# Order-only edges on the accumulating DRAM transfers of a Strassen-like FFN kernel

## The chip, the core and the metric

The kernel runs on one core of a Trainium2 chip. The metric is device time in microseconds, the median of repeated executions of the whole kernel. Engines are named as the profile names them: PE is TensorE (with PEld for its weight loads), DVE is VectorE, ACT is ScalarE, POOL is GpSimd, and SP is the engine that issues most of the DMAs.

## The reference, cut to what matters

The kernel computes one layer: a gated linear attention mixer, then a gated FFN with a short causal convolution, then a last norm. The change lies in the FFN.

```python
def causal_dwconv(u, w, b):          # K = 3
    up = jnp.pad(u, ((0, 0), (K - 1, 0), (0, 0)))
    out = up[:, K - 1:K - 1 + L] * w[K - 1] + b
    for k in range(K - 1):
        out = out + up[:, k:k + L] * w[k]
    return out

def conv_ffn(h, w_up, conv_w, conv_b, w_down):
    u = causal_dwconv(h @ w_up, conv_w, conv_b)
    g, val = jnp.split(u, 2, axis=-1)
    return (jax.nn.silu(g) * val) @ w_down
...
x = x + conv_ffn(rmsnorm(x, ffn_norm_w[i]), ...)
```

There are 2048 tokens of 1024 features, and the FFN is 2816 wide. All data are float32.

## The kernel before

Every large matrix product is made of 7 block products in place of 8 (the scheme of Strassen in Winograd's form). The products are called p1 to p7; sums and differences of blocks are formed ahead of them and after them. Each float32 operand is split into a rounded high part and a rest (`split`, L186 to L189: ACT casts the high part, DVE subtracts it), and `mm3p` (L173 to L184) makes three matmuls of each pair of operands, at L179, L180 and L181.

The FFN has an up part (`phase_u`) and a down part (the last loop of the kernel).

**The up part** goes over the tokens in two halves of 1024, called s = 0 and s = 1, and in each half over 11 groups, g or q = 0 to 10, of two blocks f = 2g and 2g + 1 of 128 FFN features. A group has 14 jobs, seven products in the order `OPS` = p1, p5, p6, p7, p4, p2, p3 with two blocks each; a job is 12 matmuls, so a group is 168. The first matmul of a group's p2 writes a tile `ub`, which is how a group is found in the trace. For every job there is a weight operand:

- `load` (L1198) has SP fetch the four blocks of the weights of each f into tiles `ur`.
- `prep` (L1207) runs five jobs ahead of PE. For p5, p6, p7 and p3 POOL forms sums of blocks: `us` at L1214 (p5), L1217 (p6), L1232 (p3), and `ur` at L1220 (p7). Then ACT casts the result into `uw` and DVE subtracts (L188 and L189).
- PE's results are copied by ACT (`c<-ua`, L1237 for p1 and p6, L1342 for p7). p1, p6, p7 and p4 of a block add up in one PSUM bank `ua`. So PE may start p6 only when ACT has copied p1's result out, and p7 only when p6's has been copied.
- `new_u` (L1240) takes a buffer `u` out of three; its first instruction, at L1243, is a copy of two columns on POOL, which waits for the convolution that held the buffer before. `conv` (L1247) is the convolution: ACT at L1253, DVE twice at L1255, and for the gating half ACT's Silu at L1257. `gated` (L1260) multiplies the two halves on DVE (L1262).

**The operands of the down part** are formed from the results of `gated`. In the second half, POOL makes four sums for each group into SBUF tiles `as` (L1284), and SP writes them out. In the first half, SP writes plain blocks into DRAM tiles `ad` (L1267), and the sums are formed in DRAM: a transfer issued on POOL's queue reads one `ad` tile and adds it to another (`gather`, L1360 to L1363). Four of these belong to each q, and each reads or writes what another one has written:

1. p7 += p5
2. p5 += p4
3. p6 += p5
4. p3 += p6

In the program they are traced during the second half, at jobs 2, 5, 10 and 13 of each group (the table `GATHER`, L1288 and L1296 to L1298); the third and the fourth of the last q are traced in the down part (L1548 and L1550). A scheduler decides where each instruction stands on its engine. It puts an instruction where its inputs are there by its own reckoning, and so the 44 transfers stand on POOL in the first half, right behind the writes that they need.

**Between the halves**, `load_op` (L900, called from L1305) has SP fetch the 28 operand tiles `h_p` of the second half, 512 KB each, while the last group of the first half runs.

**The down part** takes 14 units of 11 steps: p1, p5, p6, p7, p2, p4, p3, each for both halves. SP loads the operands `da` (L1402) eleven steps ahead.

Of the kernel before, what the change touches and what calls it, by code (L numbers as in the profile page):

```python
# [14 lines left out]
ALU = mybir.AluOpType  # L15
# [10 lines left out]
def hybrid_kernel(  # L26
# [17 lines left out]
    nc = tc.nc  # L44
# [67 lines left out]
    def scratch(shape, name):  # L112
        return dr.tile(shape, F32, tag=name, name=name)
# [10 lines left out]
    ad = {(s, o, q): scratch([P, 512], f"ad_{s}_{o}_{q}") for s in range(NS) for o in OPS for q in range(NQ)}  # L124
# [4 lines left out]
    def aux_ps(name):  # L129
        return ps.tile([P, 512], F32, tag="aux", name=name, bufs=4)  # L130
# [66 lines left out]
    halo = cst.tile([P, 2 * NF, 2], F32, name="halo")  # L197
# [984 lines left out]
    def tiles2(ap):  # L1182

        v = ap.rearrange("p (j c k) -> p c j k", c=2, k=P)
        return v[:, 0], v[:, 1]
# [6 lines left out]
    def phase_u():  # L1192
# [47 lines left out]
        def new_u(s, i, f):  # L1240
            c = f + i * NF
            u = pools["us"].tile([P, TS + 2], F32, tag="u", name=f"u_{s}_{c}", bufs=3)
            nc.gpsimd.tensor_copy(u[:, 0:2], halo[:, c, :])  # L1243
            made["u", i, f] = u
            return tiles2(u[:, 2:2 + TS])

# [48 lines left out]
        for k, (s, g, o, f) in enumerate(jobs):  # L1295
            if s == 1 and k % GJ in GATHER:  # L1296
                dst, src, back = GATHER[k % GJ]
                gather(dst, src, g - back)  # L1298
# [27 lines left out]
            elif o == "p5":  # L1326
                c = bank["c", f] = aux_ps(f"uc_{s}_{f}")
                mm3p(c, pairs)
            elif o == "p6":
                a = bank["a", f]  # L1330
                mm3p(a, pairs, first=False, more=True)
                made["u2", f] = copied(f"c2_{s}_{f}", a)
            elif o == "p2":
                pb = mm_ps(f"ub_{s}_{f}")
                mm3p(pb, pairs)
                ev, _ = new_u(s, 0, f)
                nc.vector.tensor_add(ev, tiles1(pb), tiles1(made.pop(("p1", f))))  # L1337
            elif o == "p7":
                a = bank["a", f]
                mm3p(a, pairs, first=False, more=True)  # L1340
                u3 = pools["us"].tile([P, 512], F32, tag="as", name=f"c3_{s}_{f}", bufs=AB)
                nc.scalar.copy(u3, a)  # L1342
                ev, od = new_u(s, 1, f)
                made["ev", f] = ev
                nc.vector.tensor_add(od, tiles1(bank["c", f]), tiles1(u3))
            elif o == "p4":
                a = bank.pop(("a", f))
                mm3p(a, pairs, first=False, more=True)
                nc.scalar.copy(made.pop(("ev", f)), tiles1(a))
                conv(s, 1, f)  # L1350
            else:
                c = bank.pop(("c", f))
                mm3p(c, pairs, first=False, more=True)
                _, od = tiles2(made["u", 0, f][:, 2:2 + TS])
                nc.vector.tensor_add(od, tiles1(c), tiles1(made.pop(("u2", f))))  # L1355
                conv(s, 0, f)
                gated(s, f)


    def gather(o, src, q):  # L1360

        if 0 <= q < NQ:
            nc.gpsimd.dma_start(ad[0, o, q], ad[0, src, q], accum_op=ALU.add, max_dma_last_dim=2048)  # L1363

    units = [(o, s) for o in ("p1", "p5", "p6", "p7", "p2", "p4", "p3") for s in range(NS)]
    steps = [(o, s, q) for o, s in units for q in range(NQ)]
# [163 lines left out]
    for n, (o, s) in enumerate(units):  # L1530
        banks = [(mm_ps if n % 2 == 0 else aux_ps)(f"pd_{o}_{s}_{m}") for m in range(PAIRS)]
        last = n + 1 == len(units)

        def products(q, ms):
            ah, al = aops[o, s, q]
            for m in ms:
                ts = slice(m * P, (m + 1) * P)
                mm3p(banks[m], [((ah[:, ts], al[:, ts]), wops[o, q])], first=(q == 0), last=(q == NQ - 1))

        tail = 5 if last else 0  # L1540
        for q in range(NQ):
            k = n * NQ + q
            d_load(k + DLEAD + DLOAD + 1)
            d_prep(k + DLEAD + 1)
            if n < NS and q < TT:
                load_x1(s * TT + q)
            if n == 0 and q == TT:
                gather("p6", "p5", NQ - 1)  # L1548
            elif n == 1 and q == TT:
                gather("p3", "p6", NQ - 1)  # L1550
            if n == 2 and q == 0:
                nc.sync.dma_start(nwf, final_norm_w.partition_broadcast(P))
            if q < NQ - tail:
                products(q, range(PAIRS))
        for m in range(PAIRS):
            for q in range(NQ - tail, NQ):
                products(q, [m])
            use(o, s, m, banks[m], nwf)
# [31 lines left out]
```

## Time and profile before

| | |
|---|---|
| median of three runs | 2170.98 us (2165.34 to 2174.02) |
| time of the profiled execution | 2172.34 us |
| its span | 2170.3 us |
| PE busy | 2080.6 us (96%) |
| DVE busy | 1627.6 us (75%) |
| ACT busy | 1105.6 us (51%) |
| POOL busy | 688.3 us (32%) |

The profile is that of one execution. A row of a timeline has the start in us, the duration in us, the engine with the line, the operation, and the tiles as out<-in; in brackets stands the idle time of the engine just ahead of it and what ended it. A row of a list of waits has the engine and line that waited, what it waited for, the sum in us, the number of times and the longest one. In names such as `ua<-h_p,uw_p` the numbers are left out.

### The profile page before, as it was taken

To read this page: it belongs to the slowest core of one execution; us is meant where nothing else is said; L and a number is where in the kernel's file an instruction comes from. 1 tells how busy PE (TensorE), PEld (TensorE's weight loads), DVE (VectorE), ACT (ScalarE), POOL (GpSimd) and SP (SyncE) were. 2 spreads that over 40 slices of the span, in tenths; PEclk is the share of its full clock that TensorE was granted. 3 is DMA by queue.
4 is the path that set the end of the run, shared out by engine and by line. 5 is a ranking of instruction groups with operands and counts; after the bars stand their busy time and mean duration, and the time that the engine had idled before them with its cause. 6 is when DMAs were issued, how large, how long until landed. Compare 5 with 4: busy or idle time off the path is not lost.

```text
span 2170.3 us, 28933 instructions
## 1 busy us (share of the span) xinstructions
PE 2080.6 (96%) x9832; PEld 1723.4 (79%) x9832; DVE 1627.6 (75%) x2168; ACT 1105.6 (51%) x2024; POOL 688.3 (32%) x606
## 2 busy tenths in 40 slices
PE   6999999989998998899999997999999999999998
PEld 5888788878887877688787786888888877888886
DVE  8756888799888664678988875988788777457564
ACT  5555755665565775454554543554445533233342
POOL 2000011111111002345446444665665444036010
PEclk9999999999999999999999999999999999999999
DMA  6646684578557899686676679342424567354453
GB/s 220 224 165 212 211 296 139 157 228 300 170 190 261 315 332 363 224 220 157 174 199 155 177 198 294 97 122 83 136 73 122 185 244 281 95 184 160 142 180 115
DMA packets 328357, 423.30 MB, mean 195 GB/s; under 512 B 24446, under 2 KB 183342, under 8 KB 328208
## 3 DMA queue, kind: packets, MB, share of 16 engines
q1 hardware_dynamic: 284336, 346.99, 48.8%
q10 hardware_dynamic: 37536, 62.93, 8.6%
q0 software_dynamic: 6336, 11.54, 3.5%
q8 instruction: 77, 1.26, 0.2%
q14 instruction: 72, 0.59, 0.1%
HBM read 278.23 MB, written 154.66 MB: 199 GB/s over the span
## 4 chain that ended last, share of the span: by engine, by line
PE 56%; DMA 14%; DVE 13%; issue 7%; POOL 4%; ACT 3%; SPq 2%; ACTq 0%; DVEq 0%; POOLq 0%
PE pd_p L180 5%; PE pd_p L181 5%; PE pd_p L179 5%; PE ua L179 4%; PE ua L181 4%; PE ua L180 4%; DVE t L1255 3%; DMA ad_p<-ad_p 3%; PE uc L179 2%; PE uc L181 2%; PE uc L180 2%; PE mp_R L179 2%; PE mp_R L181 2%; PE mp_R L180 2%; PE mp_A L181 1%
## 5 line engine op out<-in xcount | busy, mean ns | idle before, releaser
L179 PE MATMUL ua<-h_p,uw_p 128*128 128x512 f32 x704 | 278.6, 396 | 23.9 <-ACT c L1237 23.9
L1255 DVE SCALAR_TENSOR_TENSOR t<-u,cw,t 128x1024 f32<-128x1024 f32 x176 | 285.3, 1625 | 11.9 <-ACT t L1253 10.9
L180 PE MATMUL ua<-h_p,uw_p 128*128 128x512 f32 x704 | 276.4, 393 | 0.0
L181 PE MATMUL ua<-h_p,uw_p 128*128 128x512 f32 x704 | 276.3, 392 | 0.0
L180 PE MATMUL pd_p<-dw_p,da 128*128 128x512 f32 x616 | 240.3, 390 | 3.4 <-DVE da L189 3.4
L179 PE MATMUL pd_p<-dw_p,da 128*128 128x512 f32 x616 | 240.1, 390 | 0.6 <-DVE u L1337 0.6
L181 PE MATMUL pd_p<-dw_p,da 128*128 128x512 f32 x616 | 240.0, 390 | 0.0
L189 DVE TENSOR_TENSOR da<-da_p,da 128x512 fp32r<-128x512 f32 x154 | 133.7, 921 | 104.5 <-ACT da L188 104.4
L188 ACT CAST da<-da_p 128x512 fp32r<-128x512 f32 x154 | 85.3, 619 | 207.2 <-PE pd_p L181 147.2
L188 ACT CAST uw_p<-us 128x512 fp32r<-128x512 f32 x132 | 82.1, 622 | 203.9 <-POOL us L1217 124.3
L179 PEld LDWEIGHTS ua<-h_p,uw_p 128*128 128x128 f32 x704 | 133.5, 190 | 58.6 <-ACT c L1237 31.5
L189 DVE TENSOR_TENSOR uw_p<-us,uw_p 128x512 fp32r<-128x512 f32 x132 | 136.3, 1038 | 51.7 <-ACT uw_p L188 50.4
L189 DVE TENSOR_TENSOR uw_p<-ur,uw_p 128x512 fp32r<-128x512 f32 x176 | 143.2, 842 | 40.8 <-ACT uw_p L188 40.6
L181 PEld LDWEIGHTS ua<-h_p,uw_p 128*128 128x128 f32 x704 | 133.4, 190 | 28.2
L180 PEld LDWEIGHTS ua<-h_p,uw_p 128*128 128x128 f32 x704 | 133.6, 190 | 27.4
L179 PE MATMUL uc<-h_p,uw_p 128*128 128x512 f32 x352 | 138.1, 392 | 4.5 <-issue 4.5
L1253 ACT ACTIVATE t<-u,cw 128x1024 f32<-128x1024 f32 x88 | 109.7, 1247 | 60.9 <-DVE u L1355 53.0
L180 PE MATMUL uc<-h_p,uw_p 128*128 128x512 f32 x352 | 137.8, 392 | 0.7 <-DVE uw_p L189 0.7
L180 PEld LDWEIGHTS pd_p<-dw_p,da 128*128 128x128 f32 x616 | 115.7, 188 | 28.6 <-DVE da L189 4.7
L181 PE MATMUL uc<-h_p,uw_p 128*128 128x512 f32 x352 | 137.6, 391 | 0.0
L179 PEld LDWEIGHTS pd_p<-dw_p,da 128*128 128x128 f32 x616 | 115.7, 188 | 25.1 <-DVE u L1337 1.0
L181 PEld LDWEIGHTS pd_p<-dw_p,da 128*128 128x128 f32 x616 | 115.7, 188 | 23.8
(278 smaller groups left out, 5340.9 us busy)
## 6 DMA issues: line engine op xcount, KB each, us to landing
ur<-in_ffn_w_up_dram SPq DMA_DIRECT2D x168, 256.0 KB, 4.0
da_p<-ad_p SPq DMA_DIRECT2D x154, 256.0 KB, 4.0
h_p<-hd_p SPq DMA_DIRECT2D x56, 512.0 KB, 8.6
ad_p<-t SPq DMA_DIRECT2D x110, 256.0 KB, 3.2
x<-in_x_dram SPq DMA_DIRECT2D x32, 512.0 KB, 4.7
ch<-in_ffn_w_down_dram SPq DMA_DIRECT2D x61, 256.0 KB, 3.7
hr_A_p<-h1d_p SPq DMA_DIRECT2D x56, 256.0 KB, 2.9
hr_B_p<-h1d_p SPq DMA_DIRECT2D x56, 256.0 KB, 3.3
```

What stands on the lines that cost most here:

```text
L179: nc.tensor.matmul(ps_ap, ah, bl, start=(first and i == 0), stop=False, **kw)
L180: nc.tensor.matmul(ps_ap, al, bh, start=False, stop=False, **kw)
L181: nc.tensor.matmul(ps_ap, ah, bh, start=False, stop=(last and i == len(pairs) - 1), **kw)
L188: nc.scalar.copy(hi, src)
L189: nc.vector.tensor_sub(lo, src, f32(hi))
L1253: nc.scalar.activation(t, u[:, 2:2 + TS], AF.Identity, scale=cw[:, 2, c:c + 1], bias=cw[:, 3, c:c + 1])
L1255: nc.vector.scalar_tensor_tensor(t, u[:, k:k + TS], cw[:, k, c:c + 1], t, op0=ALU.mult, op1=ALU.add)
```

## The change

The copy of `new_u` on POOL is remembered, and each `gather` is traced inside a block that gives it an edge to the last such copy: an edge of order alone, so that the transfer stands behind that copy in POOL's queue and waits for nothing more. Nothing is computed otherwise, and no transfer is added or taken away.

```diff
         def new_u(s, i, f):
...
-            nc.gpsimd.tensor_copy(u[:, 0:2], halo[:, c, :])
+            upool["ins"] = nc.gpsimd.tensor_copy(u[:, 0:2], halo[:, c, :])
...
+    upool = {}
+
     def gather(o, src, q):
 
         if 0 <= q < NQ:
-            nc.gpsimd.dma_start(ad[0, o, q], ad[0, src, q], accum_op=ALU.add, max_dma_last_dim=2048)
+            with tc.issue_after(upool["ins"].ins):
+                nc.gpsimd.dma_start(ad[0, o, q], ad[0, src, q], accum_op=ALU.add, max_dma_last_dim=2048)
```

The order of the instructions on PE, DVE, ACT and SP is the same before and after. On POOL the 44 transfers move, and all else keeps its order. Three places show it; `-` marks what stood there before and `+` what stands there now, and the gather's line is L1363 before and L1366 after. In a name such as `ad_p_3_378` the 3 is the q; 375 to 385 are p7's tiles, 353 to 363 are p5's, 386 to 396 p4's, 364 to 374 p6's and 408 to 418 p3's.

POOL in the first half, at the group that forms the sums for the blocks f = 10 and 11, where the sums of q = 3 stood:

```order
 L1243 COPY u_8_11095<-halo 128x2
-L1363 DMA ad_p_3_378<-ad_p_3_356 128x512
-L1363 DMA ad_p_3_356<-ad_p_3_389 128x512
 L1214 TENSOR_TENSOR us_10_11098<-ur_10_0_10905,ur_10_1_11005 128x512
 L1220 TENSOR_TENSOR ur_10_0_10905<-ur_10_0_10905 128x512
-L1363 DMA ad_p_3_367<-ad_p_3_356 128x512
 L1214 TENSOR_TENSOR us_11_11119<-ur_11_0_10908,ur_11_1_11008 128x512
 L1220 TENSOR_TENSOR ur_11_0_10908<-ur_11_0_10908 128x512
-L1363 DMA ad_p_3_411<-ad_p_3_367 128x512
 L1251 COPY halo<-u_30_11002 128x2
```

All four transfers of a q are gone from between the weight sums.

POOL at the end of the first half, ahead of the first weight sums of the second half (`us_0`):

```order
 L1243 COPY u_43_12939<-halo 128x2
 L1243 COPY u_20_13010<-halo 128x2
-L1363 DMA ad_p_9_384<-ad_p_9_362 128x512
-L1363 DMA ad_p_9_362<-ad_p_9_395 128x512
-L1363 DMA ad_p_9_373<-ad_p_9_362 128x512
-L1363 DMA ad_p_9_417<-ad_p_9_373 128x512
 L1251 COPY halo<-u_42_12913 128x2
 L1251 COPY halo<-u_43_12939 128x2
```

Here the four stood in one row, each behind the one that it needs, and all four are gone.

POOL in the second half, around the weight sums for f = 10 and 11:

```order
 L1243 COPY u_9_14562<-halo 128x2
+L1366 DMA ad_p_3_411<-ad_p_3_367 128x512
 L1217 TENSOR_TENSOR us_10_14544<-us_10_14544,ur_10_0_14364 128x512
+L1366 DMA ad_p_5_380<-ad_p_5_358 128x512
+L1366 DMA ad_p_4_368<-ad_p_4_357 128x512
 L1243 COPY u_32_14760<-halo 128x2
 L1217 TENSOR_TENSOR us_11_14565<-us_11_14565,ur_11_0_14367 128x512
```

Three transfers, of three different q, now stand around the even block's p6 sum; the fourth of a group (p5 += p4) stands two copies further on, behind `u_33` and ahead of `u_10`. A transfer and the one that it needs are now most of a group apart, or, for p7 += p5 and the p5 += p4 of the same q behind it, six instructions of POOL apart.

## The prediction

> **What bounds the kernel now.** I began with the busy time of the engines by stretch, because the change touches one third of the kernel: the first token half, the passage to the second, and the second half.
>
> ```profile
> 920.00:1290.00 370.00, 359.38 (x1558) 292.66 (x1559) 311.18 (x321) 189.07 (x289) 184.84 (x182) 1.00 0.69 179
> 1290.00:1380.00 90.00, 77.57 (x323) 62.71 (x322) 59.30 (x58) 36.08 (x54) 42.13 (x38) 0.94 0.82 253
> 1380.00:1700.00 320.00, 320.00 (x1413) 265.12 (x1412) 267.15 (x253) 156.27 (x233) 195.24 (x137) 1.00 0.34 103
> ```
>
> The columns are the stretch, its length, the busy time of PE, PEld, DVE, ACT and POOL, the granted clock, the share of DMA and GB/s. In the second half PE is busy for all 320 us: it bounds that stage. In the first half PE is idle for 10.6 us of 370 and in the passage for 12.4 us of 90, so something else bounds them. Small gaps also slow the matmuls beside them, so I read what they really cost from the distance of equal places: the first matmul of `ub`, one to a group.
>
> ```profile
> 934.44 0.39 PE L179 MATMUL ub<-h_p,uw_p 128*128 128x512 f32 x1
> ...
> 1290.52 0.39 PE L179 MATMUL ub<-h_p,uw_p 128*128 128x512 f32 x1
> ...
> 1383.89 0.39 PE L179 MATMUL ub<-h_p,uw_p 128*128 128x512 f32 x1
> ...
> 1688.53 0.39 PE L179 MATMUL ub<-h_p,uw_p 128*128 128x512 f32 x1
> ```
>
> The last two are eight groups apart: 304.64 / 8 = 38.08 us for a group when PE never waits. The first two are nine groups apart: 356.08 us, which is 13.4 us over 9 x 38.08. Between them and the second half lie two groups in 93.37 us, 17.2 us over 2 x 38.08. These **30.6 us** are all that can be won here. Next, who waits in the first half:
>
> ```profile
> POOL ad_p L1363 <- DMA ad_p<-ad_p: 76.1, 20, 7.3
> ACT uw_p L188 <- POOL us L1217: 47.2, 18, 5.5
> ...
> POOL ad_p L1363 <- DMA ad_p<-t: 34.3, 9, 3.9
> ...
> PE ua L179 <- ACT c L1237: 8.8, 13, 1.7
> ```
>
> POOL stands for 110 us at its own accumulating transfers, ACT stands for POOL's weight sums, and PE stands 13 times for a copy that ACT makes late. ACT and POOL work in order, so these could be one cause. The chain of waits shows that they are:
>
> ```profile
> 1040.77 3.62 DMA ad_p<-t
> ...
> 1045.00 6.98 DMA ad_p<-ad_p
> ...
> 1052.91 1.60 POOL us L1214
> ...
> 1054.59 2.17 POOL ur L1220
> ...
> 1059.29 1.56 POOL us L1214
> ...
> 1064.52 1.25 POOL us L1217
> ...
> 1072.38 1.27 DVE t L1255
> ...
> 1080.36 3.70 DMA ad_p<-t
> ```
>
> Each row is a start, a duration and what the chain was on. It is a loop with no PE in it: a write of `gated` lands, the first transfer runs for 6.98 us while the second one waits for it at the head of POOL, then come the weight sums, the casts, the convolution and the next write. One turn takes 39.59 us, longer than PE's 38.08. That is the first half's bound. In the passage:
>
> ```profile
> 1288.80 0.84 POOL L1363 DMA_DIRECT2D ad_p<-ad_p  x1 [7.10 <-DMA h_p<-hd_p]
> ...
> 1304.16 1.56 POOL L1214 TENSOR_TENSOR us<-ur,ur 128x512 f32<-128x512 f32 x1
> ...
> 1320.96 0.80 PE L179 MATMUL ua<-h_p,uw_p 128*128 128x512 f32 x1 [7.26 <-ACT c L1237]
> ...
> 1349.96 0.77 PE L179 MATMUL uc<-h_p,uw_p 128*128 128x512 f32 x1 [4.50 <-issue]
> ```
>
> The four transfers of q = 9 stand in a row ahead of the second half's first weight sum; it starts at 1304.16, and 16.8 us later PE has stood for 7.26 us. The 4.50 us at 1349.96 are ahead of p3 of that group; the order of the program has PE wait there for the last operand tiles `h_p`.
>
> **The change part by part.** Nothing is removed but places. *First half:* 40 transfers leave the queue, 4 for each of q = 0 to 9, and the turn loses the waits between them. Take the turn above. Its first L1214 also needs weights that SP fetched behind the same writes:
>
> ```profile
> 1045.11 4.77 SPq L1204 DMA_DIRECT2D ur<-in_ffn_w_up_dram  x5
> ...
> DMA to landing us min/median/max: 6.0/6.1/6.9
> ```
>
> The second row is that of the first four of these loads. They are there from 1051 on, two of them hardly before 1052.9, so I leave the first L1214 where it is. The second L1214 can follow as soon as the L1220 ahead of it ends, at 1054.59 + 2.17 = 1056.76, and not at 1059.29: 2.5 us. The transfer ahead of L1217 goes too, 0.5 us. 39.59 - 3.0 = 36.6 us, under 38.08, so PE bounds again. Of the 13.4 us I take **12.4** as won, 1 us left for groups less regular than this one; the ends are 0 and 13.4.
>
> *Passage:* it has a second cause, and it stays.
>
> ```profile
> 1280.00:1304.00 24.00, 24.00 (x108) 19.87 (x107) 9.53 (x11) 7.24 (x11) 3.10 (x5) 1.00 1.08 323
> ...
> 1289.41 8.42 SPq L1204 DMA_DIRECT2D ur<-in_ffn_w_up_dram  x4
> ...
> DMA to landing us min/median/max: 9.6/11.5/12.2
> ```
>
> The last row is that of these four weight loads. The DMA engines are full (a share of 1.08), since the 28 `h_p` loads run here. The first weight block landed at 1289.41 + 9.6 = 1299 at the earliest, so with the loads as they are the first L1214 can move up by 5 us at most. What helps is that the transfers are DMA work too:
>
> ```profile
> q0 software_dynamic: 6336, 11.54, 3.5%
> ...
> L1363 POOL DMA_DIRECT2D ad_p<-ad_p x44: 805/813/1042, 924.0 to 1349.9; - x44
> ...
> DMA to landing us min/median/max: 3.7/6.0/8.1
> ```
>
> The queue of the transfers took 3.5% of 2170.3 us on all 16 engines, or 1.7 us for each of 44. Four fewer, ahead of 1304, free up to 7 us of a full queue, and then the loads land some 3 to 4 us sooner. After 1304 I count nothing: five transfers go, about as many come. I take 4 to 6 us off the first stop and its slow matmuls, and 2 to 4 off the second: **8 of 17.2**; the ends are 0 and 17.2.
>
> *Second half:* 44 issues come. What one holds POOL for is seen where nothing waits between it and the next instruction:
>
> ```profile
> 1052.37 0.81 POOL L1363 DMA_DIRECT2D ad_p<-ad_p  x1 [6.55 <-DMA ad_p<-ad_p]
> ```
>
> The L1214 behind it starts at 1052.91: 0.54 us. Where three of them come in:
>
> ```profile
> 1502.46 0.52 POOL L1243 COPY u<-halo 128x2 f32<-128x2 f32 x1 [1.21 <-DVE t L1255]
> 1503.01 2.28 POOL L1217 TENSOR_TENSOR us<-us,ur 128x512 f32<-128x512 f32 x1
> 1506.50 0.18 POOL L1243 COPY u<-halo 128x2 f32<-128x2 f32 x1 [1.21 <-DVE t L1255]
> 1507.65 1.68 POOL L1217 TENSOR_TENSOR us<-us,ur 128x512 f32<-128x512 f32 x1 [0.96 <-DVE uw_p L189]
> ...
> 1515.52 0.51 POOL L1243 COPY u<-halo 128x2 f32<-128x2 f32 x1 [3.01 <-ACT t L1253]
> ...
> 1516.38 0.56 ACT L1237 COPY c<-ua 128x512 f32<-128x512 f32 x1
> ...
> 1519.89 0.39 PE L179 MATMUL ua<-h_p,uw_p 128*128 128x512 f32 x1
> ```
>
> The even sum (1503.01) ends 0.54 later, at 1505.83; two issues end at 1506.91; the copy waiting until 1506.50 is 0.4 late; the odd sum still starts at 1507.65, when DVE is done. So it costs nothing on the path. If that cover goes, there is another: the odd sum ended at 1509.33, and through ACT and DVE in order it sets ACT's copy, done at 1516.94, which PE needs at 1519.89. **The margin is 2.95 us.** Behind the transfers on POOL stand only these sums and copies. The fourth stands behind `u_33`, ahead of a copy that waits for DVE anyway. None should wait for the one before it: most of a group lies between them, or, for p5 += p4, the 9 us from 1506 to the copy at 1515.52, against a median landing of 6.0. The DMA engines have room, at a share of 0.34. What the trace of before never shows is two transfers issued with none landed between. I take 0.54 us for the second; it could be as much as the 6 to 7 us of before. *Down part:* SP's queue keeps its order, and its loads of `da` come to the sums only in the third unit (p5), some 60 us after the last matmul of the up part; nothing.
>
> Sum: 2172.34 (the profiled execution; its span is 2170.3, and the median shown, 2170.98, is 1.4 lower) - 12.4 - 8 = 2151.9; from the median it would be 2150.6. I say **2151**.
>
> **The rivals.**
>
> *The loop closes another way (or the passage gives nothing).* The weight loads stand on SP behind the same writes, so the loop still exists: write, `ur` load, sums, cast, convolution. I gave it 36.6 us. If the loads land 1.5 us later than I think, nothing but a part is won. For it: DVE is busy for 311 of 370 us. Against it: the same loop in the second half, where POOL has more to do (195 of 320 us), leaves PE no gap. Price: a win of 4 to 11 us, 2161 to 2168.
>
> *It does not do what it says:* the edges hold only the order, and a transfer might still reach POOL's head unready. But a transfer can now not stand ahead of a copy in the second half, so its sources landed long ago. Price: 2172.
>
> *Slower: three transfers at a time hold POOL.* Should POOL's queue take a transfer only when the one before has landed, as its waits had it until now, then three in a row around the even sum cost 6 us for the second and 6 for the third. The second starts at 1505.8 and the first landed at 1509; the second at 1515, so the odd sum starts at 1515.6 or so instead of 1507.65: 8 us late, 5 over the margin, ten times: + 50 us. With the 20.4 won, 2202. It decides from 2.95 us of lateness on. Against it: the issues took 805 to 1042 ns, not more, but each was alone. Nothing else speaks for it.
>
> *Held by DVE.* POOL's transfers might have to wait for DVE's instructions to end.
>
> ```profile
> L1255 DVE SCALAR_TENSOR_TENSOR t<-u,cw,t 128x1024 f32<-128x1024 f32 x176 | 285.3, 1625 | 11.9 <-ACT t L1253 10.9
> ```
>
> If each of the three waited for one whole such instruction, 1.6 us, the odd sum would start at 1506.91 + 4.9 + 0.18 = 1512.0, 4.3 us late, 1.4 over the margin: 14 us in ten groups, 2166. It decides above 1.1 us each. Against it: the 44 issues had DVE busy for 84% of the time beside them, and the longest took 1042 ns where the median took 813, so 0.2 us each is what the trace bears out. The Trainium skill ("SBUF — State Buffer", in "SBUF: two separate sides") has this as a rule: GpSimd cannot write the descriptors of its own DMAs while a two-port operation of VectorE holds the port that they share, and a DMA of some 620 ns takes some 3100 ns. By that figure, as an estimate from the page, three would cost 7.4 us and ten groups some 40 us. The trace does not agree, with its 1042 ns at most.
>
> **How the numbers follow.** Forecast as above (2145 to 2160): 0.66. The loop or the passage keeps a part (2161 to 2168): 0.17. No effect: 0.06. Held by transfers in flight: 0.08. Held by DVE: 0.03. The range of 2141 to 2166 takes in the whole 30.6 us at one end, and most of the partial case and the hold by DVE at the other; outside are no effect, the transfers in flight and a little of the partial case, 0.18. About 0.5% (10.9 us) is what a measurement of this kernel can tell from no change. Faster than that are the forecast and half the partial case, 0.74; within it the other half, no effect and the hold by DVE, 0.18; slower is 0.08.
>
> **What would show it.** Right: `ub` to `ub` at 38.1 us in the first half; POOL's waits at its transfers near 0; ACT's idle time for `us` in the first half down; one stop or two left in the passage, 7 to 11 us over; in the second half PE still without a gap, and the odd L1217 at most 1 us later. Wrong: a first half still at 39 us or more, with the chain going through `ur` loads; a passage of 93 us as before; POOL standing between the three transfers, and PE waiting for L1237 in the second half.

## The result, and the profile after

| | before | after |
|---|---|---|
| median, measured side by side | 2172.11 us (2165.34 to 2174.02) | 2149.05 us (2146.11 to 2150.57) |
| the profiled execution | 2172.34 us | 2148.77 us |
| its span | 2170.3 us | 2146.8 us |

The ratio is 0.9898, with a 95% interval of 0.9873 to 0.9922: the changed kernel is faster by 1.0%, or 23 us of the medians. The forecast was 2151 us, range 2141 to 2166. In the changed kernel the lines behind `gather` are numbered three higher, so the transfers are at L1366 and the chain sums of the down part, before at L1420, at L1423.

First the busy time by stretch of the changed kernel (stretch, length, busy us of PE, PEld, DVE, ACT, POOL, granted clock, share of DMA, GB/s), with the borders moved to its own stages:

```profile
920.00:1280.00 360.00, 360.00 (x1585) 297.47 (x1584) 316.05 (x319) 189.42 (x288) 171.11 (x146) 1.00 0.55 163
1280.00:1360.00 80.00, 74.05 (x317) 60.23 (x316) 57.68 (x56) 37.76 (x57) 45.33 (x38) 0.98 0.83 250
1360.00:1680.00 320.00, 320.00 (x1413) 264.99 (x1412) 265.10 (x256) 156.51 (x232) 215.74 (x172) 1.00 0.52 128
```

PE no longer has a gap in this stretch: 360 us of 360, where it had been idle for 10.6 of 370. (One stop lies at the edge: 3.08 us at 921.81 before, inside the stretch of before, and 1.92 us at 917.86 after, just outside this one.) In the passage 6 us of gaps are left of 12.4. In the second half POOL works 20 us more and the DMA engines have a share of 0.52 in place of 0.34, and PE is as busy as it was. Then the distances of `ub`, by the timeline of PE in the changed kernel:

```profile
930.51 0.39 PE L179 MATMUL ub<-h_p,uw_p 128*128 128x512 f32 x1
...
1273.64 0.39 PE L179 MATMUL ub<-h_p,uw_p 128*128 128x512 f32 x1
...
1358.20 0.39 PE L179 MATMUL ub<-h_p,uw_p 128*128 128x512 f32 x1
...
1700.92 0.39 PE L179 MATMUL ub<-h_p,uw_p 128*128 128x512 f32 x1
```

The nine groups of the first half take 343.13 us (356.08 before), that is 0.4 over 9 x 38.08. The two groups of the passage take 84.56 (93.37 before), 8.4 over. The nine groups of the second half take 342.72, exactly 9 x 38.08, as before. From the last `ub` to the end of the span there are 445.9 us, and there had been 443.7: the down part has lost 2.2. The rest of the span's difference lies ahead of these places: 2.8 us before the first `ub`, where no transfer stands in either kernel, and 1.1 us in the group after it.

The waits of the changed kernel from 925 to 1285 (who waited, for what, us in sum, times, longest):

```profile
POOL us L1214 <- DMA ur<-in_ffn_w_up_dram: 101.9, 10, 17.2
ACT uw_p L188 <- POOL us L1217: 55.8, 15, 5.5
...
ACT uw_p L188 <- POOL us L1214: 7.0, 2, 5.8
```

POOL's 110 us at its own transfers are gone. It now waits for the weight loads, about 9 us in most groups, which harms nobody, since PE waits for nothing here. In the passage, by the timelines of POOL and PE in the changed kernel:

```profile
1280.18 1.29 POOL L1214 TENSOR_TENSOR us<-ur,ur 128x512 f32<-128x512 f32 x1 [9.83 <-DMA ur<-in_ffn_w_up_dram]
...
1297.82 0.50 PE L179 MATMUL ua<-h_p,uw_p 128*128 128x512 f32 x1 [2.26 <-ACT c L1237]
...
1324.07 0.47 PE L179 MATMUL uc<-h_p,uw_p 128*128 128x512 f32 x1 [3.09 <-DVE u L1337]
```

The first weight sum stood 13.6 us behind the passage's first `ub` (1304.16 after 1290.52); it now stands 6.5 us behind it (1280.18 after 1273.64), and it is the weight load that it waits for. That load, the first of four, is issued at 1270.03 and lands after 10.0 us, at 1280.03; before, it was issued at 1289.41 and landed after 11.5 us, at 1300.9, and the sum still stood 3.3 us behind it. Measured from `ub`, 4.0 of the sum's 7.1 us therefore come from the load and 3.1 from POOL's queue. PE's first stop went from 7.26 to 2.26 us, the second from 4.50 to 3.09.

At the start of the down part, by the timeline in order of time, POOL and DVE, first before:

```profile
1737.28 6.90 POOL L1420 TENSOR_TENSOR ch<-ch,ch 128x512 f32<-128x512 f32 x4
...
1737.80 1.85 DVE L1255 SCALAR_TENSOR_TENSOR t<-u,cw,t 128x1024 f32<-128x1024 f32 x1
```

and after, with PE:

```profile
1710.58 1.68 POOL L1366 DMA_DIRECT2D ad_p<-ad_p  x2
1711.11 7.19 DVE L1255 SCALAR_TENSOR_TENSOR t<-u,cw,t 128x1024 f32<-128x1024 f32 x1
1711.68 5.53 POOL L1423 TENSOR_TENSOR ch<-ch,ch 128x512 f32<-128x512 f32 x4
...
1718.96 0.79 PE L179 MATMUL pd_p<-dw_p,da 128*128 128x512 f32 x1 [4.96 <-DVE u L1337]
```

Before, the four chain sums and DVE's instruction got on side by side. Now two transfers are issued just ahead of the four sums, the sums run without a break, and the DVE instruction that begins beside the issues lasts until they have ended. PE stops for 4.96 us, where it had several stops of 0.6 to 1.5 us that came to 4. Behind the long stop ten matmuls start 0.43 us apart, in place of 0.23, which the short stops do not bring about: the loss is more than the difference of the stops.

### The profile page after: what moved, and what is told of

The parts are those of the page before. It is cut to its first block, busy times and chain, and to the rows that moved or that the text cites. A ratio compares the mean times of both kernels' runs of the same rounds, so it can differ in the third digit from the quotient of the medians.

```text
span 2146.8 us, 28913 instructions
## 1 busy us (share of the span) xinstructions
PE 2078.5 (97%) x9832; PEld 1726.5 (80%) x9832; DVE 1627.1 (76%) x2168; ACT 1104.8 (51%) x2024; POOL 696.2 (32%) x606
## 4 chain that ended last, share of the span: by engine, by line
PE 78%; DVE 7%; DMA 6%; issue 4%; ACT 2%; SPq 1%; POOL 1%; ACTq 0%; DVEq 0%; POOLq 0%
PE pd_p L179 7%; PE ua L179 7%; PE pd_p L180 7%; PE pd_p L181 6%; PE ua L180 6%; PE ua L181 6%; PE uc L179 3%; PE uc L181 3%; PE uc L180 3%; PE mp_Y L180 2%; PE mp_Y L181 2%; PE mp_Y L179 2%; PE ub L180 2%; PE ub L179 2%; PE ub L181 2%
## 5 line engine op out<-in xcount | busy, mean ns | idle before, releaser
L1255 DVE SCALAR_TENSOR_TENSOR t<-u,cw,t 128x1024 f32<-128x1024 f32 x176 | 277.5, 1581 | 7.7 <-ACT t L1253 6.7
L189 DVE TENSOR_TENSOR da<-da_p,da 128x512 fp32r<-128x512 f32 x154 | 130.7, 901 | 104.4 <-ACT da L188 102.3
L189 DVE TENSOR_TENSOR uw_p<-ur,uw_p 128x512 fp32r<-128x512 f32 x176 | 156.4, 914 | 41.1 <-ACT uw_p L188 41.0
L179 PEld LDWEIGHTS ua<-h_p,uw_p 128*128 128x128 f32 x704 | 133.2, 189 | 38.3 <-ACT c L1237 10.6
L189 DVE TENSOR_TENSOR uw_p<-us,uw_p 128x512 fp32r<-128x512 f32 x132 | 119.5, 914 | 47.2 <-ACT uw_p L188 46.7
```

What stands on the lines that cost most here:

```text
L179: nc.tensor.matmul(ps_ap, ah, bl, start=(first and i == 0), stop=False, **kw)
L189: nc.vector.tensor_sub(lo, src, f32(hi))
L1255: nc.vector.scalar_tensor_tensor(t, u[:, k:k + TS], cw[:, k, c:c + 1], t, op0=ALU.mult, op1=ALU.add)
```

## The experiments

For each kernel the same places were read, the first matmuls of `ub`. The table has the nine groups of the first half, the two of the passage, the nine of the second half, the time from the last `ub` to the end of the span, and the median. The kernels with one copy and three copies and the one with the transfers among the chain sums were timed once.

| | first half | passage | second half | to the end | time, us |
|---|---|---|---|---|---|
| before | 356.08 | 93.37 | 342.72 | 443.7 | 2172.11 |
| after | 343.13 | 84.56 | 342.72 | 445.9 | 2149.05 |
| `e_first_late` | 344.15 | 84.34 | 342.72 | 444.2 | 2149.18 |
| `e_left_out` | 343.08 | 81.08 | 342.72 | 441.1 | 2142.93 |
| `e_edges_q0_8` | 343.31 | 94.03 | 342.72 | 444.1 | 2157.88 |
| `e_edges_q9_10` | 356.74 | 82.21 | 342.72 | 448.6 | 2163.84 |
| `e_copy1` | 343.09 | 84.41 | 344.08 | 448.0 | 2152.81 |
| `e_copy3` | 343.13 | 85.74 | 361.95 | 447.2 | 2173.21 |
| `e_tail_after` | 343.15 | 84.28 | 342.72 | 443.4 | 2144.62 |
| `e_tail_mid` | 342.75 | 81.35 | 343.36 | 448.1 | 2153.13 |
| `e_clear` | 344.81 | 83.40 | 342.72 | 441.6 | 2144.07 |
| `e_first_one` | 351.20 | 90.88 | 342.72 | 443.0 | 2159.57 |

A passage of the same instructions differs by some us between kernels: `e_tail_mid` has up to 1380 the order of the changed kernel and 81.35, 3.2 us less than it. Differences of that size in one place of two kernels are not argued from. For the time to the end all twelve kernels can be taken together: the five with transfers directly ahead of the chain sums, or among them, lie at 445.9 to 448.6 us, the seven without at 441.1 to 444.2.

**Are the waits the cause, or the place?** `e_first_late` leaves the transfers in the first half, where they lay before, but two groups later.

```diff
-            if s == 1 and k % GJ in GATHER:
+            if k % GJ in GATHER:
                 dst, src, back = GATHER[k % GJ]
-                gather(dst, src, g - back)
+                gather(dst, src, s * NQ + g - back - 2)
...
-            if n == 0 and q == TT:
-                gather("p6", "p5", NQ - 1)
-            elif n == 1 and q == TT:
-                gather("p3", "p6", NQ - 1)
```

> The edges of the changed kernel stay, but the 44 transfers stand two groups behind the writes of their sums: those of q = 0 to 8 in the first half again, those of q = 9 and 10 at the passage and in the first two groups of the second half; none in the down part. THEORY (what cost the time was POOL standing at the head of its queue before transfers whose data had not landed): two groups later the data has landed, so POOL waits for nothing, although first half, POOL and DMAs carry the same transfers as in the kernel before. First half 343 +- 2 us for its nine groups (38.1 each, before 356.1); passage 84 to 91 us (about three transfers more in it than in the changed kernel, at up to 1.7 us of all DMA engines each); total 2146 to 2157. RIVAL (the place costs: traffic of the transfers or their issue time in the first half, where loads of weights run besides): first half 350 us or more, total 2158 to 2172.

The first half takes 344.15 us, and the whole is as fast as the changed kernel (ratio to before 0.9905, interval 0.9888 to 0.9921). With 33 of the 44 transfers in the first half, next to nothing is lost. POOL's longest waits, in the list of `e_first_late` from 930 to 1276, are these:

```profile
POOL us L1214 <- DMA ur<-in_ffn_w_up_dram: 93.0, 9, 16.6
...
POOL u L1243 <- DVE t L1255: 29.3, 13, 2.9
```

The transfers are not in the list at all. So the second half as a place gives nothing that two groups do not. But the two groups change two things at once: a transfer finds its data landed when POOL reaches it, and it no longer runs beside the loads for which the next sums wait. The first transfer of a q is issued 17 to 19 us ahead of `ub` here, and 8.5 to 10.5 us ahead before the change, just as SP issues those loads.

**Which of the waits?** `e_first_one` puts the transfers one group later. The first two of each q then stand where they stood before the change, and the third and fourth come a group later.

```diff
-                gather(dst, src, s * NQ + g - back - 2)
+                gather(dst, src, s * NQ + g - back - 1)
```

(The lines with a minus are those of `e_first_late`.)

> The transfers stand one group behind the writes in place of two. By the order of instructions the first two (p7<-p5, p5<-p4) then stand just where they stood before the change, at the head of POOL ahead of the first L1214; only the third and fourth, which stood between the weight sums, are a group later. THEORY (as the prediction's step on the first half has it: the first L1214 waits for its ur loads anyway, and only the transfers between the sums, 2.5 + 0.5 us of a turn of 39.59 us, make the turn longer than PE's 38.08): POOL still waits 3 to 4 and 6 to 7 us at the two first transfers, but 38.1 to 38.4 us per group, first half 343 to 346 us, total 2146 to 2152. RIVAL (it is the two long waits ahead of the sums that count): 39 us or more per group, first half 351 us or more, total over 2157.

The result lies between the two. The first half takes 351.20 us, 8.1 over the changed kernel's and just over the rival's bound. In its list of waits from 935 to 1275:

```profile
POOL ad_p L1366 <- DMA ad_p<-ad_p: 50.1, 8, 7.1
POOL ad_p L1366 <- DMA ad_p<-t: 35.1, 9, 4.2
...
PE ua L179 <- ACT c L1237: 4.0, 6, 2.1
```

The two long waits ahead of the first weight sum remain, 85 us in sum. How much goes with them depends on where one begins to count. Over all nine groups it is 8.1 of 13 us, and moving the third and fourth transfer alone gives 4.9 (356.08 - 351.20). But half of the 8.1 lies in the first of the nine groups: it takes 42.12 us here and 39.29 before, and the group ahead of it 45.87 here and 48.51 before, so the two together took as long as before. The other eight groups took 316.79 us before, take 309.08 here (38.6 each, where 38.1 to 38.4 or 39 and more had been expected) and 305.05 in the changed kernel: there the third and fourth transfer give 7.7 of 11.7 us and the first two hold 4.0. The prediction had given all of it to the third and fourth. The step that was wrong is that the first L1214 stays where it is because of its loads: it stood 0.7 us ahead of `ub` in the group at 1053.65 (1052.91), and in the changed kernel, in the group at 1121.32, it stands 3.7 us ahead:

```profile
1117.63 1.51 POOL L1214 TENSOR_TENSOR us<-ur,ur 128x512 f32<-128x512 f32 x1 [9.15 <-DMA ur<-in_ffn_w_up_dram]
```

It still waits for its load, but the load lands sooner. SP issues it at nearly the same distance from `ub` (the last five loads of these two groups begin at 1045.11 and 1112.03, 8.5 and 9.3 us ahead), but it takes less time. By the view of the line of the loads from 930 to 1265, first before, then `e_first_one`, `e_first_late` and after:

```profile
DMA to landing us min/median/max: 3.0/6.0/9.8
...
DMA to landing us min/median/max: 3.0/6.6/12.9
...
DMA to landing us min/median/max: 3.0/4.6/6.3
...
DMA to landing us min/median/max: 3.0/4.5/6.3
```

The three kernels that issue a transfer 8 to 11 us ahead of `ub` in these groups, beside the loads (before, `e_first_one` and `e_edges_q9_10`), have medians of 6.0 to 6.6 us; the nine others have 4.4 to 4.8. In `e_first_one` the corresponding sum, at 1126.41 for a `ub` at 1126.77, is only 0.4 ahead. As these traces read, the first transfer delays the first sum twice, at POOL's head and by its traffic beside the loads; no run takes these two apart.

**One loss or two?** In `e_edges_q0_8` the edges hold only the transfers of q up to 8, in `e_edges_q9_10` only the others.

```diff
-            with tc.issue_after(upool["ins"].ins):
+            with (tc.issue_after(upool["ins"].ins) if q < NQ - 2 else ExitStack()):
```

> The edges hold only the transfers of q = 0 to 8; those of q = 9 and 10 stand where they stood before, four and four in a row in the two groups of the passage. THEORY (two separate losses): first half as in the changed kernel, 343 +- 2 us; passage as before, 90 to 95 us; down part as before, 443 to 445; total 2154 to 2160. RIVAL (the passage was late only because it inherited the lateness of the first half): passage 83 to 87 us, total 2145 to 2151.

> The edges hold only the transfers of q = 9 and 10; those of q = 0 to 8 stand where they stood before, in the first half, in front of the sums. THEORY (two separate losses): first half as before, 354 to 358 us for nine groups, POOL again waiting at its transfers; passage as in the changed kernel or a little less (no transfers of q = 0 in it), 82 to 86 us; down part 444 to 446; total 2160 to 2166. RIVAL (the first half's loss came from something else than these transfers, or the passage depends on the first half): first half 343 to 350 or passage over 90.

(For the second, `q >= NQ - 2`.) The two kernels take the gain apart as forecast: with q up to 8 held, the first half is that of after (343.31) and the passage that of before (94.03); with q = 9 and 10 held it is the other way (356.74 and 82.21). The passage did not inherit its lateness. `e_edges_q9_10` takes 448.6 us to the end, where 444 to 446 had been expected: it has the same long DVE instruction at the start of the down part, 7.16 us, and PE stops there for 6.72 us. Of `e_edges_q0_8`, POOL's timeline in the passage shows what it is:

```profile
1274.29 0.81 POOL L1366 DMA_DIRECT2D ad_p<-ad_p  x1 [6.46 <-DMA h_p<-hd_p]
...
1281.59 0.83 POOL L1366 DMA_DIRECT2D ad_p<-ad_p  x1 [6.49 <-DMA ad_p<-ad_p]
1282.38 1.58 POOL L1214 TENSOR_TENSOR us<-ur,ur 128x512 f32<-128x512 f32 x1
```

Again the transfers of q = 9 stand ahead of the first weight sum and wait, 6.46 and 6.49 us, and the sum comes 11.7 us behind `ub` (at 1270.67), where it comes 6.5 behind in the changed kernel.

**What do the transfers still cost?** `e_left_out` leaves them out, and so the sums of the first half.

```diff
-            if s == 1 and k % GJ in GATHER:
-                dst, src, back = GATHER[k % GJ]
-                gather(dst, src, g - back)
...
-            if n == 0 and q == TT:
-                gather("p6", "p5", NQ - 1)
-            elif n == 1 and q == TT:
-                gather("p3", "p6", NQ - 1)
```

> The 44 transfers and their edges are left out, so the sums of the first token half are not completed in DRAM. THEORY (in the changed kernel the transfers lie hidden in the second half, five of them cost a little in the passage, and three of them cost about 2 us in the down part): second half again 38.08 us per group; passage 78 to 84.6 us; from the last ub to the end 441 to 444 us (445.9 in the changed kernel, 443.7 before); total 2138 to 2147. RIVAL (what is left of the passage over two groups at 38.08 comes from the loads alone): passage 84.6 +- 1, total 2146 to 2149. RIVAL (the issues cost POOL time that the second half feels): second half below 38.08 us per group, which PE's own busy time there speaks against.

The second half stays at 342.72: there the 44 issues cost nothing. The passage keeps 4.9 us over 76.16 without any transfer, so at least that much is not theirs. To the end there are 4.8 us less than in the changed kernel. By the medians, all 44 together cost the kernel before, measured beside this one at 2169.91, some 27 us, and the changed kernel some 6 (2149.05 - 2142.93). The second figure compares medians that were not measured side by side; by the ratios to before, 0.9898 and 0.9878, it is some 4, and their intervals overlap.

**How large is the margin in the second half?** One copy and three copies of the odd sum onto itself ahead of the odd L1217.

```diff
+                if s == 1 and f % 2 == 1:
+                    for _ in range(1):
+                        with tc.issue_after(upool["ins"].ins):
+                            nc.gpsimd.tensor_copy(src, src)
                 sub(src, src, a11)
```

> The changed kernel with one copy of the odd sum onto itself (128x512, on POOL, 1.3 to 1.8 us as the sums there) in each group of the second half, held behind the last u copy and ahead of the odd L1217. THEORY (the prediction's margin: the odd L1217 may come 2.95 us later before PE feels it, of which the transfers' issues have used up to 1 us): still 38.08 us per group in the second half. RIVAL (the issues had already used the margin up): 39 us or more per group.

> As the run with one copy, with three copies per group; by the order of instructions the even L1232 also comes ahead of the odd L1217, so that this stands 5.2 to 6.9 us later. THEORY (margin 2 to 2.95 us): each group of the second half 2.3 to 4.9 us longer, 40.4 to 43 us, and PE idle there until ACT's cast of the odd sum. RIVAL (POOL has slack of over 7 us there, so the margin was far larger than predicted): again 38.08 us.

In the group at 1472.44 of the changed kernel the odd L1217 starts 9.5 us behind `ub`. With one copy it starts 13.3 us behind in every group, 3.7 later and not only 1.3 to 1.8, and still seven of the nine groups take 38.08 to 38.10 us; two take 38.7, each with one stop of 0.32 us (`e_tail_mid`, without any copy, has one group like that). With three copies it starts 17.7 us behind in most groups, 8.2 later and not the 5.2 to 6.9 expected, and five of the nine groups take 40.0 to 40.4 us (the others 38.1, 39.6 and 41.9 twice). There PE waits where the prediction had it, for ACT's copies (PE's timeline of `e_copy3`; its lines are four higher again, so L1241 is L1237 of before):

```profile
1465.39 0.50 PE L179 MATMUL ua<-h_p,uw_p 128*128 128x512 f32 x1 [0.90 <-ACT c L1241]
...
1471.53 0.50 PE L179 MATMUL ua<-h_p,uw_p 128*128 128x512 f32 x1 [0.36 <-ACT c L1241]
```

So the margin is real and the path is the one named, but it is at least 3.7 us, not 2.95. 8.2 us late for 1.9 us a group would put it at some 6 us, an estimate from these two offsets; the one group of 38.1 agrees with it, since there the odd L1217 starts 15.4 us behind, 5.8 later. The granted clock of `e_copy3` is 0.941 where the others have 0.988 to 0.994. In the groups of 40.0 us only the first matmuls behind a stop are slower (0.34 us in place of 0.23), so its two stops make up the 1.9 us there; in the groups of 41.9 us a stretch of matmuls is slow too, and these I leave out of the estimate.

**The loss in the down part.** `e_tail_after` has the last three transfers behind the first five chain sums; `e_tail_mid` has them among these.

```diff
-                nc.gpsimd.tensor_sub(chain[q], r[0], chain[q])
+                upool["ins"] = nc.gpsimd.tensor_sub(chain[q], r[0], chain[q])
...
-                gather(dst, src, g - back)
+                if (dst, g - back) != ("p3", NQ - 2):
+                    gather(dst, src, g - back)
...
-            if n == 0 and q == TT:
+            if n == 2 and q == 0:
+                gather("p3", "p6", NQ - 2)
                 gather("p6", "p5", NQ - 1)
-            elif n == 1 and q == TT:
+            elif n == 2 and q == TT:
                 gather("p3", "p6", NQ - 1)
```

> The changed kernel with its last three transfers (p3<-p6 of q = 9 and 10, p6<-p5 of q = 10) behind the five first chain sums of the down part in place of ahead of four of them. THEORY (two transfer issues just ahead of four POOL sums in a row held a DVE operation for 7.19 us; before the change the same four sums shared with DVE and it took 1.85 us): the DVE operation 1.2 to 2.4 us, no PE gap of 5 us; from the last ub to the end 442.5 to 444.5 us (445.9 in the changed kernel); total 2145 to 2148. RIVAL (the 5 us gap comes from the transfers' own DMA traffic in front of the loads of the down part, or from any other cause): 445 us or more wherever they stand.

```diff
-            if n == 0 and q == TT:
+            if n == 1 and q == TT:
                 gather("p6", "p5", NQ - 1)
-            elif n == 1 and q == TT:
+            elif n == 2 and q == TT:
                 gather("p3", "p6", NQ - 1)
```

> The changed kernel with its last three transfers spread among the chain sums: sum, u copy, transfer, sum, transfer, three sums, transfer. THEORY (a DVE operation that starts while POOL issues a transfer, with sums in a row behind it, is held until those sums end): if DVE starts one during the second issue, held by the three sums behind it for about 1.2 + 3 x 1.25 = 5 us; otherwise 1.2 to 2.4 us. From the last ub to the end 443 to 446 us. RIVAL (any transfer in this place costs the same): again 7 us held and 446 us.

Behind the sums the transfers cost nothing: 443.4 us to the end, as before the change, no stop of PE beyond 2.1 us, and the DVE instruction is short again (timeline of DVE, `e_tail_after`):

```profile
1709.09 2.15 DVE L1255 SCALAR_TENSOR_TENSOR t<-u,cw,t 128x1024 f32<-128x1024 f32 x1
```

Among the sums I had expected a hold of at most 5 us, and it is 7.17, with 448.1 us to the end: that is near what the rival had (7 us and 446). The timeline of `e_tail_mid`, POOL and DVE, shows how the theory can still stand:

```profile
1714.60 0.83 POOL L1366 DMA_DIRECT2D ad_p<-ad_p  x1
1715.14 7.17 DVE L1255 SCALAR_TENSOR_TENSOR t<-u,cw,t 128x1024 f32<-128x1024 f32 x1
1715.17 1.56 POOL L1423 TENSOR_TENSOR ch<-ch,ch 128x512 f32<-128x512 f32 x1
1716.40 1.11 POOL L1366 DMA_DIRECT2D ad_p<-ad_p  x1
1716.97 4.25 POOL L1423 TENSOR_TENSOR ch<-ch,ch 128x512 f32<-128x512 f32 x3
```

DVE's instruction begins beside the first issue, not the second, and is then held by everything that POOL runs without a break: the sum, the second issue and three sums, to 1721.2. The start that I had assumed was wrong. With the right one the hold agrees with the theory, but this run does not separate it from the rival; what speaks against the rival's "any transfer in this place" is `e_tail_after` alone.

**Together.** `e_clear` traces the transfers of q up to 7 and the first two of q = 8 in the first half, two groups late, leaves the passage out and does the rest from the third group of the second half.

```diff
-            if s == 1 and k % GJ in GATHER:
+            if k % GJ in GATHER and (s == 0 or g > 1):
                 dst, src, back = GATHER[k % GJ]
-                gather(dst, src, g - back)
+                gather(dst, src, (s * (NQ - 2) + g) - back - 2)
...
-            if n == 0 and q == TT:
-                gather("p6", "p5", NQ - 1)
-            elif n == 1 and q == TT:
-                gather("p3", "p6", NQ - 1)
```

> All 44 transfers, held by edges, but none in the passage and none in the down part: those of q up to 8 in the first half, two groups behind the writes, the rest from the third group of the second half on. THEORY (POOL's waits gone; the transfers in the passage cost 3 us there, those ahead of the chain sums 2 us in the down part): first half 343 to 344.5 us, passage 79 to 82.5 us, second half 342.7 us, from the last ub to the end 441 to 444.3 us; total 2141 to 2146, faster than the changed kernel by 3 to 8 us. RIVAL (the passage's 3 us between the changed kernel and the one without transfers were chance): passage 84 us, total 2146 to 2149.

2144.07 us, ratio to before 0.9882 (0.9864 to 0.9899). The down part gains as forecast (441.6). One transfer, the last of q = 7, still came in the passage, at 1284.94. The passage is 83.40, outside the 79 to 82.5 of the theory and within what chance gives, so whether transfers in the passage cost anything is not settled. `e_clear` and `e_tail_after` have the lowest times of the kernels that compute everything. The intervals of their ratios overlap with that of the changed kernel, so that they beat it is likely from the down part (2.5 to 4.3 us less) and not shown by the times alone.

## Why the prediction was right

- **First half:** forecast 12.4 us won, measured 12.95. The bound, the loop through POOL, was right, and the size came out, but the working behind it was in part luck. I held the first L1214 in place and gave the gain to the transfers between the sums alone. `e_first_one` takes those away and wins 4.9 of 13 (7.7 of 11.7 without its first group); the rest goes with the two transfers ahead of the first L1214, which delay it at POOL's head and delay its load as well. I had taken the landing of the loads as given, and it went from a median of 6.0 to 4.5 us. The whole came out right because the change moves all four, and PE's own 38.08 us caps what a group can win.
- **Passage:** forecast 8 of 17.2 us, measured 8.8. The first stop went by 5.0 (forecast 4 to 6), the second by 1.4 (forecast 2 to 4). That a second cause stays was right: 4.9 us are left even without any transfer. The weight loads of the first sums land in 8.7 to 10.0 us, before in 9.6 to 12.2. One reading was off: of the four loads I took the shortest, 9.6 us, and allowed the first L1214 5 us; the first load took 11.5 us, so with the loads as they were only 3.3 us were there. The loads came 4.0 us sooner (forecast 3 to 4), by flights 1.5 us shorter and an issue 2.5 us further ahead of `ub`.
- **Second half:** forecast nothing, measured nothing, and of three transfers in a row none waited: the changed kernel's transfers have these durations (ns: least, median, most), idle times and landings.

```profile
L1366 POOL DMA_DIRECT2D ad_p<-ad_p x44: 782/818/1137, 1283.4 to 1717.7; - x44
...
  DMA ad_p<-ad_p: 0.5, 1
...
DMA to landing us min/median/max: 3.7/4.7/7.1
```

  One wait of 0.5 us in 44 refutes the rival in which three in flight hold POOL, and a longest issue of 1137 ns the one in which DVE holds it. The margin was undersized: at least 3.7 us for 2.95.
- **Down part:** forecast nothing; measured a loss of 2.2 us. This is the step that was plainly wrong. I looked at SP's queue and at the `da` loads that need the transfers, and not at what stands behind the last three on POOL, the chain sums, nor at who works beside those, DVE.
- **Signs named ahead:** all came true; the odd L1217 starts 8.7 to 10.7 us behind `ub` in the second half, before 9.5 to 11.3, so it is not late at all. ACT's idle time for `us` fell as a sum, and not in both its parts: in the lists from 925 to 1285 of after, 55.8 for L1217 and 7.0 for L1214, before (920 to 1290) 47.2 and 43.7.
- **The sum:** the terms give 12.95 + 8.8 - 2.2 = 19.5 us, forecast 20.4. The other 3.9 us of the span's 23.5 lie ahead of the first half. 2.8 of these come before any transfer, where the kernels of the table, which have the same instructions there, reach the first `ub` between 881.4 and 887.9 us; so these 2.8 us cannot be put down to the change, and how much of the medians' 23 us is of that kind these single profiles do not show.

## What to carry to other kernels

A transfer that waits at the head of an in-order queue costs what stands behind it, and, as the landings here read, its traffic delays the loads beside it; moving it need not mean moving it far: in the first half two groups later did as much as eleven, and one group did a part only, because the first two transfers still stood, and ran, where they had been. When an issue is moved, look at what runs on the same engine directly behind the new place and at the engine that works beside that, not only at the one who needs the data. And when several waits of one loop are removed together, the sum can be right with the gain put down to the wrong ones; only taking them away apart tells.

## What the runs showed of the hardware

At the start of the down part, a DVE instruction that began beside a transfer's issue on POOL, with chain sums directly behind the issue, lasted until 0.6 to 1.1 us after POOL's unbroken run ended. It is seen in all five kernels that have transfers directly ahead of, or among, the chain sums: 7.19 us (after), 7.16 (`e_edges_q9_10`), 7.17 (`e_tail_mid`), 6.74 (`e_copy1`), and 5.50 with three sums in the run (`e_copy3`). In the two kernels with copies it is another instruction, DVE's subtraction at L189. The other seven kernels have the same sums without an issue ahead, and the instruction takes 1.85 to 2.15 us there; the four sums take 6.90 us in place of 5.53 (before and after), with DVE's instructions between them. It is no rule for every issue with sums behind it. In the first half of the kernel before, the instruction of 1093.02 began beside an issue too and was held by one sum only: it ended while POOL's second sum ran (timelines of POOL and DVE).

```profile
1092.49 0.81 POOL L1363 DMA_DIRECT2D ad_p<-ad_p  x1 [7.22 <-DMA ad_p<-ad_p]
1093.04 1.58 POOL L1214 TENSOR_TENSOR us<-ur,ur 128x512 f32<-128x512 f32 x1
1094.70 2.17 POOL L1220 TENSOR_TENSOR ur<-ur 128x512 f32<-128x512 f32 x1
...
1093.02 2.69 DVE L1255 SCALAR_TENSOR_TENSOR t<-u,cw,t 128x1024 f32<-128x1024 f32 x1 [0.45 <-ACT t L1253]
```

The Trainium skill ("SBUF — State Buffer", in "SBUF: two separate sides") says that a VectorE instruction with two SBUF inputs and a GpSimd instruction that reads SBUF exclude each other at a shared pair of ports: whichever starts first has the pair for the whole instruction, and the other one is blocked. The alternation, and the hold by one sum, agree with it. A hold over four GpSimd instructions does not follow from it; why the pair isn't handed over between them there, no run here shows.

Weight loads that were issued beside an accumulating transfer landed later: the medians are 6.0 to 6.6 us in the three kernels that have one there and 4.4 to 4.8 us in the nine that do not.
